# Phase 1 of a bidirectional scan layer: two scan operands per tile and store, with other places for three intermediates

## The chip, the cores and the metric

The kernel runs on one core of a Trainium2 chip. The metric is device time in microseconds of one execution. A core has TensorE (matrix products, into the accumulator memory PSUM), VectorE, ScalarE and GpSimd for elementwise work on the on-chip memory SBUF, and SyncE, which here issues most of the DMA transfers. Each engine has its own queue of instructions; they wait for one another by semaphores.

## What is computed

One layer for 128 context tokens and 2048 latent tokens of width 1024. A normalised and modulated input `h` goes through one projection to r, k, v and gate channels (group A, 8 heads of 64) and to the four inputs of a gated convolution (group B). Group A is a delta-rule scan in both directions:

```
kk = k * kk_scale / norm;  kd = k * (1 + (a - 1) * ka_scale)
S  = S * w_t - (S kk_t) (kk_t * a_t)^T + v_t k_t^T ;   y_t = S r_t
y  = groupnorm(y_fwd + y_bwd) * gn_w + gn_b + bonus * v,   bonus = sum(r * kd * bonus_rk)
out = x + gate * ([y * silu(g_a), yb] @ w_out)
```

The decay `w` and the rate `a` differ per direction and come from two small low-rank products of `h`. The outputs are the normalised results and the final states of the context.

## The kernel before

There are three phases, all written for one core. Phase 1 makes everything that depends on one token block alone and writes it to DRAM; phase 2 runs the scan in chunks of 64 tokens; phase 3 does the output projection. The Tile framework takes the program's tiles, gives them places in SBUF and decides the order of the instructions on each engine from a simulated timeline; waits follow from the tiles. A tile names a pool, a tag and a number of places (`bufs`); the tiles of one tag take turns in its places, and a new tile waits until the last reader of the old one, a store among them, is done.

**Phase 1** (`phase1`, lines 50 to 644) takes the 2176 tokens in six blocks (five of 384, one of 256), two blocks at a time: three "thirds" (`THIRD`, the loop at line 571). In each third the weights are walked once: for each of four groups of 128 channels, `turn(0, ...)` runs `mixA` on both blocks and `turn(1, ...)` runs `gateA`, with the convolution's `convB` and `gateB` between them. Each product is made of three matmuls per 128 input channels, with weights and inputs split into a high and a low part (`products`, lines 158 to 162).

`load_w` (line 117) brings a weight column block. The first time it loads raw weights into a place of tag "wr" (pool `wp`, 2 places of 4 KB in each partition), ScalarE and VectorE split them, and the two parts are stored to DRAM (`scr_wsp`); in the later thirds both parts are loaded from there, 1 MB at a time (line 121), so "wr" is used in the first third only. `gate_rows` (line 528) uses it there too.

`mixA` (lines 337 to 411) makes, for one channel group and token block, the shifted k (line 345) and r (line 356, through `shifted`, lines 313 to 330, in which ScalarE empties the product's PSUM place at lines 319 and 321 and GpSimd adds neighbours at line 323), the normalised k (lines 346 to 355, with a sum over the heads by `part_sum`), and then for each direction d the four operands of the scan: al (line 387), rh (line 390), ka (line 398) and be (lines 401 and 402). Each of the four is a tile [128, 384] of tag "sp", which has four places, and each has a store of its own through `spill` (line 332), issued by SyncE into one of four planes of the DRAM tensor `ops0` or `ops1`. The bonus sum over both directions ends in a tile "bsum" (lines 405 to 410).

`gateA` (lines 413 to 444) makes the shifted v (line 418), transposes it on TensorE (line 422) and writes it less its head mean into a tile "vt" (one place, line 423; line 432), stored at line 433. The low part in `parts_of` (line 195) has the same tag "vt". Then comes the gate sg, and the term q = (bonus * v + bias) * sg, in another "sp" tile (lines 441 to 443), with a store.

At the end of the third third, phase 1's pools on the right side are closed (line 632) and phase 2's first tiles take their room: `early` (line 1153) loads masks, makes the operand tiles rr (preset at line 787) and loads the scan operands of the first two stages (line 868), with the initial states ahead of them (line 948). The convolution's last two groups run beside it.

Of the kernel before, what the change touches and what calls it, by code (L numbers as in the profile page):

```python
# [6 lines left out]
F32 = mybir.dt.float32  # L7
# [9 lines left out]
BLK = [(0, 384), (384, 384), (768, 384), (1152, 384), (1536, 384), (1920, 256)]  # L17
# [10 lines left out]

OPS = dict(al0=0, rh0=1, ka0=2, be0=3, be1=0, ka1=1, rh1=2, al1=3)


class Ctx:
# [15 lines left out]
def phase1(K):  # L50
    nc, tc, A, S = K.nc, K.tc, K.A, K.S
    V, G, P, T = nc.vector, nc.gpsimd, nc.scalar, nc.tensor
    cp = Pool(K, "p1c", "left")
    wp = Pool(K, "p1w", "left", 2)
# [4 lines left out]
    ta_ = Pool(K, "p1ta", "right")  # L59
# [36 lines left out]
    def vcol(i):  # L96
        return vec[:, i:i + 1]
# [15 lines left out]
                up[n, d] = (hi[:, n, d], lo[:, n, d])  # L113

    kept = set()

    def load_w(cb):

        w = wp.tile([128, 2, 8, 128], F32R, tag="w", name=f"w{cb}_{K.u()}", bufs=4)
        if cb in kept:  # L120
            nc.sync.dma_start(w[:].bitcast(F32), S["wsp"][cb])
            return w
        raw = wp.tile([128, 8, 128], F32, tag="wr", name=f"wr{cb}_{K.u()}", bufs=2)
        nc.sync.dma_start(raw[:], A["win"][cb])
        P.copy(w[:, 0], raw[:])
        V.tensor_tensor(w[:, 1], raw[:], w[:, 0].bitcast(F32), ALU.subtract)
        nc.sync.dma_start(S["wsp"][cb], w[:].bitcast(F32))
        kept.add(cb)
        return w
# [23 lines left out]
    def dense(w, hh, n, nm):  # L153
        ps = pmm.tile([128, 384], F32, tag="mm", name=f"mm{nm}_{K.u()}")
        products(ps, w, hh, n, range(8))
        return ps
# [174 lines left out]

    def spill(name, g, j, t_, nm):
        t0, n = BLK[j]
        dst = S[f"ops{name[2]}"][OPS[name]] if name in OPS else S[name]
        nc.sync.dma_start(dst[g * 128:(g + 1) * 128, t0:t0 + n], t_[:, :n])

    def mixA(g, j, ws, hh, lw, pre):

        t0, n = BLK[j]
        nch = n // 64  # L340
        tl = lambda tag, b=1: (tp if tag == "sg" else ta_).tile([128, 384], F32, tag=tag, name=f"{tag}_{g}_{j}_{K.u()}", bufs=b)
        wk, wr_ = ws
        psk, psr = pre or (None, None)

        kS = shifted(psk or dense(wk, hh, n, "k"), j, 1, g, "k", 1)
        sq = tl("sq")
        P.activation(sq[:, :n], kS[:, :n], AF.Square, scale=vcol(V_KK + g))
        pss = part_sum(onr, sq, n, f"s{g}_{j}")
        n2 = sq
        V.tensor_scalar(n2[:, :n], pss[:, :n], 1e-24, None, ALU.max)  # L350
        V.reciprocal(n2[:, :n], n2[:, :n])
        kk = tl("kk")
        P.activation(kk[:, :n], kS[:, :n], AF.Identity, scale=vcol(V_KK + g))
        kkn = n2
        V.tensor_tensor(kkn[:, :n], kk[:, :n], n2[:, :n], ALU.mult)
        rS = shifted(psr or dense(wr_, hh, n, "r"), j, 0, g, "r", 1)
        kds = []
        for d in range(2):
            cs = slice(g * 128, g * 128 + 128)

            def lup(which):
                ps = pmm.tile([128, 384], F32, tag="mm", name=f"up{which}_{K.u()}")
                hi, lo = up[which, d]
                x = lw[which * 2 + d]
                T.matmul(ps[:, :n], hi[:, cs], x[:, :n], start=True, stop=False)
                T.matmul(ps[:, :n], lo[:, cs], x[:, :n], start=False, stop=True)
                return ps

            psw = lup(0)
            t = tl("t", 2)  # L370
            P.activation(t[:, :n], psw[:, :n], AF.Tanh, bias=dcol(D_W0H + d * 4 + g), scale=0.5)
            V.tensor_scalar(t[:, :n], t[:, :n], -0.5 * DEC, -0.5 * DEC, ALU.mult, ALU.add)
            c = t
            if d == 0:
                V.tensor_tensor_scan(c[:, :n], smask[:, :n], t[:, :n], 0.0, ALU.mult, ALU.add)
            else:
                V.tensor_tensor_scan(c[:, :n][:, ::-1], smask[:, :n], t[:, :n][:, ::-1], 0.0, ALU.mult, ALU.add)
            pt = rot(pp[d], "pp")
            c3 = c[:, :n].rearrange("p (a b) -> p a b", b=64)
            P.activation(pt[:, :nch, 1 - d:65 - d], c3, AF.Exp)  # L380
            P.activation(c[:, :n], c[:, :n], AF.Exp, bias=nln2[:], scale=-1.0)
            psa = lup(1)
            ta = tl("ta", 2)
            P.activation(ta[:, :n], psa[:, :n], AF.Tanh, bias=dcol(D_IBH + d * 4 + g), scale=0.5)
            v3 = lambda x_: x_[:, :n].rearrange("p (a b) -> p a b", b=64)
            al = tl("sp", 4)
            V.tensor_tensor(v3(al), v3(kk), pt[:, :nch, d:64 + d], ALU.mult)
            spill(f"al{d}", g, j, al, "al")
            rh = tl("sp", 4)
            V.tensor_tensor(v3(rh), v3(rS), pt[:, :nch, 1 - d:65 - d], ALU.mult)  # L390
            spill(f"rh{d}", g, j, rh, "rh")
            nc.scalar.dma_start(S[f"pc{d}"][g * 128:(g + 1) * 128, t0 // 64:t0 // 64 + nch], pt[:, :nch, 64 - 64 * d])

            kd = tl("kd", 2)
            P.activation(kd[:, :n], ta[:, :n], AF.Identity, bias=dcol(D_KA2 + g), scale=vcol(V_KA + g))
            V.tensor_tensor(kd[:, :n], kd[:, :n], kS[:, :n], ALU.mult)
            kap = tl("sp", 4)
            V.tensor_tensor(kap[:, :n], kd[:, :n], c[:, :n], ALU.mult)
            spill(f"ka{d}", g, j, kap, "kap")
            be = tl("sp", 4)  # L400
            V.scalar_tensor_tensor(be[:, :n], ta[:, :n], 1.0, kkn[:, :n], ALU.add, ALU.mult)
            V.tensor_tensor(be[:, :n], be[:, :n], c[:, :n], ALU.mult)
            spill(f"be{d}", g, j, be, "be")
            kds.append(kd)
        bs = kds[0]
        V.tensor_tensor(bs[:, :n], kds[0][:, :n], kds[1][:, :n], ALU.add)
        V.scalar_tensor_tensor(bs[:, :n], bs[:, :n], dcol(D_RKQ + g), rS[:, :n], ALU.mult, ALU.mult)
        psb = part_sum(onr, bs, n, f"b{g}_{j}")
        bsum = tl("bsum", 2)
        P.copy(bsum[:, :n], psb[:, :n])  # L410
        return bsum

    def gateA(g, j, ws, hh, bsum):

        t0, n = BLK[j]
        tl = lambda tag, b=1: (tp if tag == "sg" else ta_).tile([128, 384], F32, tag=tag, name=f"{tag}_{g}_{j}_{K.u()}", bufs=b)
        wv, wg = ws
        vS = shifted(dense(wv, hh, n, "v"), j, 2, g, "v", 1)

        psv = pax.tile([128, 3, 128], F32, tag="ax", name=f"psv{g}_{j}")  # L420
        for i in range(n // 128):
            T.transpose(psv[:, i, :], vS[:, i * 128:(i + 1) * 128], idt[:])
        vt = ta_.tile([128, 3, 128], F32, tag="vt", name=f"vt{g}_{j}", bufs=1)

        c0 = 1 if lat_off(j) else 0
        if c0:
            P.copy(vt[:, 0], psv[:, 0])
        heads = lambda x: x[:, c0:n // 128].rearrange("p i (h c) -> p i h c", h=2)
        m = n // 128 - c0
        mn = ta_.tile([128, 3, 2], F32, tag="vmean", name=f"vmean{g}_{j}", bufs=1)  # L430
        V.tensor_reduce(mn[:, :m], heads(psv), mybir.AxisListType.X, ALU.add)
        V.scalar_tensor_tensor(heads(vt), mn[:, :m].unsqueeze(3).broadcast_to((128, m, 2, 64)), -1.0 / 64, heads(psv), ALU.mult, ALU.add)
        nc.sync.dma_start(S["vt"][t0:t0 + n, g * 128:(g + 1) * 128].rearrange("(a p) c -> p a c", p=128), vt[:, :n // 128])

        psg = dense(wg, hh, n, "g")
        tg = tl("sg", 2)
        P.activation(tg[:, :n], psg[:, :n], AF.Tanh, scale=0.5)
        sg = tg
        V.scalar_tensor_tensor(sg[:, :n], tg[:, :n], 1.0, psg[:, :n], ALU.add, ALU.mult)
        spill("sg", g, j, sg, "sg")  # L440
        q = tl("sp", 4)
        V.tensor_tensor(q[:, :n], bsum[:, :n], vS[:, :n], ALU.mult)
        V.scalar_tensor_tensor(q[:, :n], q[:, :n], dcol(D_GBH + g), sg[:, :n], ALU.add, ALU.mult)
        spill("q", g, j, q, "q")
# [120 lines left out]
    def coming(j, j2):  # L565

        yield from norm_steps(j, load_x(j))
        yield from make_h(j, xb[j])
        yield from norm_steps(j2, load_x(j2))

    for t3, js in enumerate(THIRD):
        wd, wi = wlora if t3 == 0 else (load_w(32), load_w(33))
        lws, pre, conv, sums = {}, {}, {}, {}
        more = coming(*THIRD[t3 + 1]) if t3 < 2 else iter(())
        WA, WB = ((4, 0), (8, 12)), ((20, 24), (28, 16))
        early = gate_rows() if t3 == 0 else iter(())
# [837 lines left out]
```

## Time and profile before

| | us |
|---|---|
| median of three runs | 1746.37 |
| lowest and highest of the three | 1745.83, 1748.89 |
| span of the profiled execution, first to last instruction | 1752.9 |
| TensorE busy in that span | 1647.9 (94%) |
| VectorE busy | 1093.0 (62%) |
| ScalarE busy | 870.1 (50%) |
| GpSimd busy | 582.1 (33%) |

The profile was taken on one execution; its page gives the span and no other time for it, and the span is 6.5 us above the median of the runs. Times in the profile's rows count from the start of that span. The borders of the thirds lie near 390 and 717 us, and phase 2's first products are at 943 us. In a row of a timeline stand the start, the duration, the engine, the line, the operation and the tiles (written <- read), and in brackets the idle time of the engine before it and what ended that. In a row of waits stand who waited and for whom, the sum in us, how often, and the longest. In a row of windows stand the stretch, its length, the busy time (and number of instructions) of TensorE, its weight loads, VectorE, ScalarE and GpSimd, and then the granted clock of TensorE as a share of full speed, the busy share of the DMA engines, and GB/s.

### The profile page before, as it was taken

The page shows a single profiled execution, that of the slowest core. Times are in us where ns is not written, and L with a number is a line of the kernel's source. Part 1 is how long each engine was busy: PE and PEld are TensorE (multiplying, and loading weights), DVE is VectorE, ACT ScalarE, POOL GpSimd, SP SyncE. Part 2 cuts the span into 40 slices and gives each one's busy share as a digit, 9 for nine tenths or more (in the row PEclk, how much of TensorE's full clock was granted, in tenths as well). Part 3 has the DMA queues.
Part 4 walks back from the last instruction along what each step waited for, and adds up shares of the span by engine and source line. Part 5 has one row for each costly group of instructions (what it writes and reads, how often), then busy time and mean ns, then how long its engine had stood idle before and what let it go on. Part 6 is the DMA issues. An engine that isn't in the chain of part 4 may idle for free. (4 is left out here: it accounts for less than half of the span.)

```text
span 1752.9 us, 33041 instructions
## 1 busy us (share of the span) xinstructions
PE 1647.9 (94%) x12400; PEld 1558.8 (89%) x12400; DVE 1093.0 (62%) x2092; ACT 870.1 (50%) x1719; POOL 582.1 (33%) x1089
## 2 busy tenths in 40 slices
PE   5999899998999999999998989999999999899998
PEld 2889898998999998999998979899999999787886
DVE  5875788866567766567764544475776666656333
ACT  4534455534143433334442367687788787633222
POOL 0011111111011101011120587777777778223221
PEclk9899999999999999999999998899999999999999
DMA  9797778785557646477666585587677875746442
GB/s 367 208 234 220 233 241 246 232 255 151 148 160 227 169 147 174 135 258 217 195 214 225 173 196 135 141 192 187 174 198 189 191 185 120 180 151 206 151 144 90
DMA packets 315825, 335.69 MB, mean 192 GB/s; under 512 B 166985, under 2 KB 263881, under 8 KB 301585
## 3 DMA queue, kind: packets, MB, share of 16 engines
q1 hardware_dynamic: 243360, 324.52, 62.6%
q10 hardware_dynamic: 70944, 4.60, 2.9%
q0 software_dynamic: 1360, 4.46, 0.7%
q8 instruction: 98, 1.61, 0.4%
q14 instruction: 63, 0.51, 0.1%
HBM read 221.42 MB, written 112.08 MB: 190 GB/s over the span
## 5 line engine op out<-in xcount | busy, mean ns | idle before, releaser
L934 POOL TENSOR_TENSOR zt<-zt,ztmp 128x30 f32<-128x30 f32 (+7 forms) x510 | 197.3, 387 | 39.3
L1054 PE MATMUL psS<-sv,E 128*128 128x64 f32 x1088 | 155.1, 277 | 1.0 <-DVE sv L1067 0.6
L1029 PE MATMUL psE<-str,stl 128*128 128x128 f32 x1088 | 144.1, 281 | 11.3 <-DVE E L1030 7.0
L1054 PEld LDWEIGHTS psS<-sv,E 128*128 128x128 f32 x1088 | 145.4, 200 | 3.3 <-DVE sv L1067 0.8
L1029 PEld LDWEIGHTS psE<-str,stl 128*128 128x128 f32 x1088 | 131.8, 194 | 14.1 <-DVE E L1030 7.9
L931 POOL TENSOR_TENSOR ztmp<-ab,zt 128x60 f32<-128x60 f32 (+7 forms) x255 | 130.8, 513 | 19.2
L1067 DVE TENSOR_TENSOR sv<-psS,pc 64x128 f32<-64x128 f32 x254 | 69.2, 277 | 92.9 <-PE psS L1054 92.2
L779 ACT COPY bd<-rr 64x512 f32<-64x512 f32 x136 | 84.0, 617 | 75.7 <-DMA rr<-scr_ops 23.3
L323 POOL TENSOR_TENSOR shk<-rawl 128x384 f32<-128x384 f32 (+1 forms) x24 | 20.7, 861 | 291.9 <-ACT rawl L319 291.9
L1030 DVE TENSOR_TENSOR E<-psE,msk 128x512 f32<-128x512 f32 x136 | 92.7, 684 | 33.0 <-PE psE L1029 32.3
L892 PE MATMUL psF<-rr,bd 128*128 128x128 f32 x544 | 80.0, 295 | 16.2 <-ACT Q L779 9.8
L892 PEld LDWEIGHTS psF<-rr,bd 128*128 128x128 f32 x544 | 70.7, 203 | 20.4 <-ACT Q L779 12.9
L1350 POOL TENSOR_TENSOR z<-z,x 128x512 f32<-128x512 f32 x32 | 43.6, 1364 | 126.6 <-DVE z L1346 105.9
L1018 PE MATMUL psX<-F,zb 128*128 128x128 f32 x544 | 78.2, 297 | 3.2 <-ACT zb L777 2.3
L197 POOL TENSOR_TENSOR hslb<-kd,hshb 128x384 fp32r<-128x384 f32 (+1 forms) x24 | 26.7, 1113 | 164.0 <-ACT hshb L196 143.5
L160 PE MATMUL mmc<-h,w 128*128 128x384 f32 (+1 forms) x192 | 67.9, 354 | 13.4 <-ACT q1r L321 9.8
L323 POOL TENSOR_TENSOR shv<-rawl 128x384 f32<-128x384 f32 (+1 forms) x24 | 25.4, 1060 | 153.4 <-ACT rawl L319 153.4
L892 PE MATMUL psG<-rr,bd 128*128 128x128 f32 x544 | 72.0, 280 | 4.4 <-DVE F L893 4.4
L1018 PEld LDWEIGHTS psX<-F,zb 128*128 128x128 f32 x544 | 71.6, 209 | 4.0 <-POOL zt L934 1.9
L892 PEld LDWEIGHTS psG<-rr,bd 128*128 128x128 f32 x544 | 65.7, 193 | 5.0 <-DVE F L893 4.8
L161 PE MATMUL mmc<-h,w 128*128 128x384 f32 (+1 forms) x192 | 66.1, 344 | 0.0
L162 PE MATMUL mmc<-h,w 128*128 128x384 f32 (+1 forms) x192 | 65.7, 342 | 0.0
(307 smaller groups left out, 5205.4 us busy)
## 6 DMA issues: line engine op xcount, KB each, us to landing
w<-scr_wsp SPq DMA_DIRECT2D x68, 1024.0 KB, 7.3
scr_wsp<-w SPq DMA_DIRECT2D x34, 1024.0 KB, 6.0
rr<-scr_ops SPq DMA_DIRECT2D x64, 512.0 KB, 4.6
scr_ops<-sp SPq DMA_DIRECT2D x160, 192.0 KB, 5.2
wr<-in_win SPq DMA_DIRECT2D x34, 512.0 KB, 6.3
ab<-scr_at SPq DMA_DIRECT2D x34, 256.0 KB, 4.2
x<-in_x SPq DMA_DIRECT2D x17, 512.0 KB, 3.8
wadas<-in_wada SPq DMA_DIRECT2D x8, 1024.0 KB, 13.0
```

The source lines that it names most:

```text
L160: T.matmul(ps[:, :n], w[:, 0, k], hh[:, 0, k, :n], start=k == 0, stop=False)
L161: T.matmul(ps[:, :n], w[:, 0, k], hh[:, 1, k, :n], start=False, stop=False)
L162: T.matmul(ps[:, :n], w[:, 1, k], hh[:, 0, k, :n], start=False, stop=k == 7)
L779: (V.tensor_copy if k in ON_DVE else P.copy)(dst, src)
L892: T.matmul(ps[:, i, :].rearrange("p (a b) -> p a b", b=64), w[:, u, :], x[:, :, u, :], start=True, stop=True)
L931: G.tensor_tensor(tv, ab[:, j:j + 2, j + 2:32].unsqueeze(1).broadcast_to((128, kn, 2, n)), zt[:, :kn, j:j + 2].unsqueeze(3).broadcast_to(( ...
L934: G.tensor_tensor(zt[:, :kn, j + 2:32], zt[:, :kn, j + 2:32], tv[:, :, r], ALU.subtract)
L1018: T.matmul(px[:, i, :], B.zb[:, gi, us.start + i, :], g.F[:, us.start + i, :], start=True, stop=True)
L1029: T.matmul(pe[:, i, hd, :].rearrange("p (b t) -> p b t", b=2), g.lt[:, :, hd, us.start + k + i].rearrange("p b t -> p (b t)"), g.rt[:, :, ...
L1030: V.tensor_tensor(g.E[n][:, k:k + 2].rearrange("p a b c -> p (a b) c"), pe[:].rearrange("p a b c -> p (a b) c"), B.msk[:, ME[g.d]].unsquee ...
L1054: T.matmul(sp[gi][:, q, hd, :], g.E[n][:, k, hd, :], sv[:, u, hd, :], start=True, stop=True)
L1067: r = V.tensor_tensor(dst, sp[gi][0:64, q], B.pc[0:64, d, 2 * p:2 * p + 2, c:c + 1].broadcast_to((64, 2, 64)), ALU.mult)
```

## The change

The four scan operands of a direction become two tiles [128, 2, 384], a pair of al and rh and a pair of ka and be, each with one store that writes two neighbouring planes of `ops0` or `ops1`. The halves of a pair are ordered by direction so that the planes are the same as before. Tag "sp" has two places of pairs, which take the room of the four single ones. q is written into bsum's tile in place. From the second third on (`late`), every other pair, which is the al/rh pair of each direction, is a tile of tag "wr" in the pool `wp`, and so is the transposed v (two places for both). No arithmetic changes.

```diff
+    late = []
...
     def spill(name, g, j, t_, nm):
         t0, n = BLK[j]
-        dst = S[f"ops{name[2]}"][OPS[name]] if name in OPS else S[name]
-        nc.sync.dma_start(dst[g * 128:(g + 1) * 128, t0:t0 + n], t_[:, :n])
+        nc.sync.dma_start(S[name][g * 128:(g + 1) * 128, t0:t0 + n], t_[:, :n])
+
+    npair = [0]
+
+    def pair():
+
+        npair[0] += 1
+        nm = f"pair{npair[0]}"
+        if late and npair[0] % 2:
+            return wp.tile([128, 2, 384], F32, tag="wr", name=nm, bufs=2)
+        return ta_.tile([128, 2, 384], F32, tag="sp", name=nm, bufs=2)
+
+    def spill2(d, k, g, j, t_):
+        t0, n = BLK[j]
+        nc.sync.dma_start(S[f"ops{d}"][k:k + 2, g * 128:(g + 1) * 128, t0:t0 + n].rearrange("k p t -> p k t"), t_[:, :, :n])
...
-            al = tl("sp", 4)
+            ar = pair()
+            al, rh = ar[:, d], ar[:, 1 - d]
             V.tensor_tensor(v3(al), v3(kk), pt[:, :nch, d:64 + d], ALU.mult)
-            spill(f"al{d}", g, j, al, "al")
-            rh = tl("sp", 4)
             V.tensor_tensor(v3(rh), v3(rS), pt[:, :nch, 1 - d:65 - d], ALU.mult)
-            spill(f"rh{d}", g, j, rh, "rh")
+            spill2(d, 2 * d, g, j, ar)
...
-            kap = tl("sp", 4)
+            kb = pair()
+            kap, be = kb[:, d], kb[:, 1 - d]
             V.tensor_tensor(kap[:, :n], kd[:, :n], c[:, :n], ALU.mult)
-            spill(f"ka{d}", g, j, kap, "kap")
-            be = tl("sp", 4)
             V.scalar_tensor_tensor(be[:, :n], ta[:, :n], 1.0, kkn[:, :n], ALU.add, ALU.mult)
             V.tensor_tensor(be[:, :n], be[:, :n], c[:, :n], ALU.mult)
-            spill(f"be{d}", g, j, be, "be")
+            spill2(d, 2 - 2 * d, g, j, kb)
...
-        vt = ta_.tile([128, 3, 128], F32, tag="vt", name=f"vt{g}_{j}", bufs=1)
+        vt = (wp if late else ta_).tile([128, 3, 128], F32, tag="wr" if late else "vt", name=f"vt{g}_{j}", bufs=2 if late else 1)
...
-        q = tl("sp", 4)
+        q = bsum
         V.tensor_tensor(q[:, :n], bsum[:, :n], vS[:, :n], ALU.mult)
...
+        if t3:
+            late.append(t3)
```

More of the change, by code (lines that the diff above doesn't have):

```diff
@@ L27 @@
 ND = 68
-OPS = dict(al0=0, rh0=1, ka0=2, be0=3, be1=0, ka1=1, rh1=2, al1=3)
 class Ctx:
```

## The prediction

> **What bounds the kernel now.** I read the page first, then the table of windows over the three thirds of phase 1, then the waits of VectorE and TensorE in them, and last the timelines around the longest TensorE gaps.
>
> ```profile
> span 1752.9 us, 33041 instructions
> ...
> PE 1647.9 (94%) x12400; PEld 1558.8 (89%) x12400; DVE 1093.0 (62%) x2092; ACT 870.1 (50%) x1719; POOL 582.1 (33%) x1089
> ```
>
> TensorE is busy for 94% of the span, so a gain can only be TensorE idle time, or time at a lower clock. The change touches phase 1 alone, which ends near 940 us. Its thirds, with TensorE first after the length, and granted clock, DMA share and GB/s last:
>
> ```profile
> 60.00:390.00 330.00, 312.51 (x1704) 295.87 (x1703) 248.96 (x440) 151.55 (x285) 44.89 (x42) 0.97 0.80 233
> 390.00:717.00 327.00, 312.09 (x1762) 308.78 (x1761) 204.75 (x372) 117.08 (x235) 41.95 (x42) 0.98 0.59 174
> 717.00:930.00 213.00, 209.38 (x1413) 207.49 (x1412) 139.54 (x280) 83.03 (x189) 37.07 (x48) 1.00 0.65 201
> ```
>
> TensorE idles 17.5, 14.9 and 3.6 us. VectorE has room, but waits for the stores that free its four "sp" places. First third, then the other two:
>
> ```profile
> DVE sp L387 <- DMA scr_ops<-sp: 17.3, 6, 5.0
> DVE sp L401 <- DMA scr_ops<-sp: 6.1, 3, 3.5
> DVE sp L390 <- DMA scr_ops<-sp: 2.4, 3, 1.4
> ```
>
> ```profile
> DVE t L372 <- ACT t L371: 33.3, 10, 3.6
> DVE ok L329 <- POOL shk L323: 24.5, 7, 4.6
> DVE sp L387 <- DMA scr_ops<-sp: 20.0, 6, 6.7
> DVE sp L401 <- DMA scr_ops<-sp: 19.5, 11, 2.9
> DVE sp L398 <- DMA scr_ops<-sp: 10.0, 5, 3.6
> ```
>
> That is 25.8 us and 49.5 us of VectorE waiting. What TensorE waited for, first third and then the others:
>
> ```profile
> PE pss L204 <- ACT hshs L196: 4.9, 3, 3.9
> ...
> PE psb L204 <- ACT hshb L196: 1.2, 1, 1.2
> ```
>
> ```profile
> PE mmc L160 <- ACT q1r L321: 9.6, 4, 4.9
> PE psb L204 <- ACT hshb L196: 3.4, 1, 3.4
> ...
> PE pss L204 <- ACT hshs L196: 1.3, 2, 0.9
> ```
>
> ScalarE is named, but it is not the cause. Followed back, the longest gap reads:
>
> ```profile
> 428.25 0.56 DVE L398 TENSOR_TENSOR sp<-kd,t 128x384 f32<-128x384 f32 x1 [1.60 <-DMA scr_ops<-sp]
> 429.74 0.56 DVE L401 SCALAR_TENSOR_TENSOR sp<-ta,sq 128x384 f32<-128x384 f32 x1 [0.93 <-DMA scr_ops<-sp]
> ```
>
> ```profile
> 430.87 0.61 ACT L347 ACTIVATE sq<-ok,vec 128x384 f32<-128x384 f32 x1 [4.78 <-DVE ok L329]
> ```
>
> ```profile
> 432.88 0.69 PE L160 MATMUL mmc<-h,w 128*128 128x384 f32 x1 [4.87 <-ACT q1r L321]
> ```
>
> VectorE stands twice on a store, so `ok` is late; ScalarE runs its queue in order (square, scaled copy, then the copies that empty r's PSUM bank), so the next product has no bank. I followed the other gaps of the three rows back in the same way; they led to an L387, L398 or L401 wait as well.
>
> Why are stores slow to land? The issue list gives size and median time to landing:
>
> ```profile
> w<-scr_wsp SPq DMA_DIRECT2D x68, 1024.0 KB, 7.3
> ...
> rr<-scr_ops SPq DMA_DIRECT2D x64, 512.0 KB, 4.6
> scr_ops<-sp SPq DMA_DIRECT2D x160, 192.0 KB, 5.2
> ```
>
> A 192 KB store takes longer than a 512 KB load of two rows: it lands when the megabytes of weights ahead of it on the same queue have.
>
> Each gap also costs clock. Around the gaps named, with TensorE's granted clock third from the end:
>
> ```profile
> 178.00:190.00 12.00, 7.96 (x32) 7.48 (x32) 9.36 (x19) 8.74 (x18) 2.08 (x2) 0.72 0.75 276
> ...
> 286.00:296.00 10.00, 8.26 (x38) 7.61 (x37) 7.76 (x16) 2.73 (x6) 1.76 (x1) 0.84 0.95 364
> ...
> 430.00:440.00 10.00, 7.12 (x32) 7.12 (x33) 7.36 (x13) 8.27 (x17) 2.47 (x2) 0.83 0.71 221
> ```
>
> A stretch of 10 us at 0.83 lost 1.7 us. The other two long gaps of the second third (at 517 and 689) have a stretch of half clock like it, taken at the same price as an estimate: 5.1 us in the three.
>
> **The change, part by part.**
>
> *Two later thirds: four pairs.* From the second third on, the al/rh pairs go to the two "wr" places and the ka/be pairs keep the two of "sp": eight halves for four. The next writer of a place comes a whole block later, not half a block. Each third has eight blocks (four channel groups, two token blocks), so one every 27 us or more on average (213/8), though the two of a turn stand closer; with 5.2 us for a store I cost the sp waits of these thirds at nothing. The cover is that distance; if it were gone we are back at the old waits. The idle time behind them is 9.6 + 3.4 + 1.3 = 14.3 us. What is late next is ScalarE's tanh (L372's row) and GpSimd's shift sum (L329's), both of which belong to the chain of a block's start; I let them keep a fifth. So 11.5 us of idle and four fifths of the clock, 4 us: **−15.5 us**. Bounds: −19.4 (all of it) and −5 (the waits go, the gaps stay mostly).
>
> The Trainium skill, "TensorE: Matmul & The Clock Gate", Part 1, says that the clock is gated in windows of 3413 ns at half rate after an idle window. By it a gap costs 1.7 us of matmul time whatever its own length, three of them 5.1 us; the 0.83 over 10 us agrees.
>
> *The end of phase 1: the transposed v.* Its one place "vt" becomes the two "wr" places, in a pool that phase 2's first loads don't overlap; q moves from "sp" into bsum's place. Before:
>
> ```profile
> 928.66 0.42 DVE L432 SCALAR_TENSOR_TENSOR vt<-vmean,psv 128x256 f32<-128x256 f32 x1 [4.31 <-DMA scr_vt<-vt]
> 935.80 0.76 DVE L787 COPY rr<-I 128x512 f32<-128x512 f32 x2 [6.72 <-DMA scr_vt<-vt]
> ```
>
> ```profile
> SPq L948 <- DMA scr_q<-sp: 5.8, 1, 5.8
> ```
>
> ```profile
> 929.11 0.37 SPq L433 DMA_DIRECT2D scr_vt<-vt  x1
> 935.38 0.52 SPq L948 DMA_DIRECT2D st<-in_st  x1
> 936.08 1.99 SPq L868 DMA_DIRECT2D rr<-scr_ops  x4
> ```
>
> ```profile
> 943.16 1.19 PE L892 MATMUL psF<-rr,bd 128*128 128x128 f32 x4 [5.88 <-DMA rr<-scr_ops]
> ```
>
> The last v block waits for the first one's store, the preset of phase 2's operand tile waits for the last one's, the state load ahead of the operand loads on SyncE's queue waits for q's, and TensorE pays 5.88 us. Both holders move, so the loads could go some 6 us earlier; two weight loads of 1 MB are still ahead of them, at 7.3 us. I take half of the gap and 1 us of clock: **−4 us**, bounds 0 and −8. If q's store now holds back another phase 2 tile on bsum's place, it is 0.
>
> *First third: two pairs.* "wr" is still in use for raw weights, so four single places become two of pairs. The al/rh pair of the second direction waits for a store issued one VectorE instruction later than before, which is +0.5 us where it waits (six times, 3 us). Worse is the other pair: ka of the second direction used to go into any single place that was free; now it needs a whole pair, and the ka/be pair of the first direction is full only after its second product:
>
> ```profile
> 289.77 0.55 DVE L402 TENSOR_TENSOR sp<-sp,t 128x384 f32<-128x384 f32 x1
> ...
> 291.17 0.55 DVE L398 TENSOR_TENSOR sp<-kd,t 128x384 f32<-128x384 f32 x1
> ```
>
> The first row completes that pair at 290.3; with the 5.2 us of a store it lands at 295.5 by estimate, and the second row, ka of the second direction at 291.17, would start 4.3 us later. That happens once in each of eight blocks: 0 to 34 us of new VectorE waiting. The queue behind it is whatever the scheduler has interleaved (at 291 the convolution's taps), and ScalarE and TensorE wait for that. Price for TensorE: the 25.8 us of the first third's sp waits stand behind 4.9 + 1.2 us of idle and 3.4 + 1.6 us of clock (0.72 over 12 us, 0.84 over 10), about 0.4 us for each. I take 9 us from the ka pairs (a quarter of the bound, since the scheduler can place the write later) and 3 from the al pairs: 12 × 0.4 = **+5 us**, bounds −1 (fewer issues) and +15.
>
> The Trainium skill, "DMA: Bandwidth & Descriptors", Anatomy of one DMA, says that a transfer costs about 2.0 us fixed and its bytes at 436 GB/s. By it, as an estimate, a pair's store lands in 2.9 us against 2.5 for a single one, and the new wait would be near 2 us where I put 4.3; the trace's 5.2 us for 192 KB differs, since these stores queue.
>
> *Small.* q in bsum's place: its writer stands where it stood, and the next bsum copy comes a block and more later, so its cover is that distance; 0. SyncE issues 96 two-row stores for 192, as the operand loads already do; its queue is off the path; 0. A merged store is one VectorE instruction later in SyncE's queue, and the weight loads behind it with it: 0.5 us against loads made four places ahead; 0.
>
> **Sum.** −15.5 − 4 + 5 = −14.5 us. The profiled execution's span, 1752.9, lies 6.5 us above the runs' median of 1746.37; 0.4% of these terms is under 0.1 us, so I take the sum off the median: **1732 us**. Its own range, from half the first gain to all of both with no loss: 1719 to 1742.
>
> **Rivals.**
> *The gaps refill.* TensorE's gaps at a block's start have other late comers, 33.3 us of waits for the tanh and 24.5 us for the shift sum; if these come up to where the sp waits were, the first term is −5, the second −2, and the first third takes +5: 1744 us, no change. For it: those rows are longer than the sp rows. Against: at 432.88 VectorE's two waits make half of the gap by themselves.
> *The first third turns it.* Two pair places in the stage with the highest DMA share (0.80) and the busiest VectorE (249 of 330 us): with all bounds at their bad ends, −5 + 0 + 15 = +10: 1756 us. It decides once new VectorE waiting there is over 19.5/0.4 = 49 us (some 6 us a block), or less where the gains fall short. Against it: the scheduler may place the blocked write behind other work.
> *Stores land by their own size.* If a pair's place comes free 2 us after its second half, the first third costs +1, not +5, and both gains stand in full, 19.4 + 6: 1722 us. For it: in quiet stretches stores do land faster. Against: the 5.2 us row.
> *The late places aren't there.* vt and the al/rh pairs share two places; were each pair to meet a v store, the first term halves; this lies inside the forecast's range.
>
> **How the numbers follow.** Forecast 0.55, refill 0.20, first third 0.15, fast stores 0.10. Within 0.2%, about what a measurement of this kernel can tell from no change, is 1742.9 to 1749.9. Faster: the forecast, nearly all, the fast stores, and some of refill: 0.67. Same: the rest of refill and a sliver of the forecast: 0.16. Slower: 0.17. The range takes the fast stores' case and the bounds down to 1717, and goes up past refill to 1750; the bad end of the first third is left out.
>
> **What would show it.** Right: no L387 or L398 wait for a store after 400 us, the gaps at 432, 517, 593 and 688 gone, TensorE's idle time in the two later thirds under 8 us, clock 0.99 there; operand loads at the end of phase 1 right behind the weight loads and the first psF gap under 3 us; in the first third longer waits of L398. Wrong: sp waits of over 45 us in the first third with TensorE idle over 30 us there, or the same idle in the later thirds under other names.

## The result, and the profile after

The changed kernel takes 1731.63 us in the median of four runs (1725.37 to 1736.05), against 1746.1 for four of the kernel before (1745.32 to 1748.89); the medians are 14.5 us apart. The ratio is 0.9894, 95% interval 0.9864 to 0.9924: faster by 18.5 us of 1746, at least 13 and at most 24. In two later comparisons it is 0.9901 (0.9867 to 0.9935) and 0.9875 (0.9848 to 0.9902). The kernel before itself was at 1736.9, 1737.6 and 1751.7 us in later comparisons, on three different chips, so times are set side by side within one comparison only.

The page of the changed kernel, first lines:

```profile
span 1728.5 us, 32831 instructions
...
PE 1643.7 (95%) x12400; PEld 1558.1 (90%) x12400; DVE 1102.0 (64%) x2092; ACT 869.9 (50%) x1719; POOL 585.0 (34%) x1089
```

The same work stands in a shorter span. The table of windows over the thirds of phase 1, the first length after the stretch being followed by TensorE's busy time:

```profile
60.00:390.00 330.00, 312.27 (x1681) 296.53 (x1680) 248.56 (x438) 150.90 (x284) 44.73 (x42) 0.96 0.78 228
390.00:717.00 327.00, 324.07 (x1863) 322.40 (x1862) 215.96 (x384) 119.56 (x241) 42.52 (x43) 1.00 0.63 183
717.00:930.00 213.00, 208.28 (x1424) 206.94 (x1423) 148.74 (x289) 85.02 (x193) 39.73 (x47) 0.99 0.70 223
```

In the second stretch TensorE's idle time went from 14.9 to 2.9 us and its clock from 0.98 to 1.00. (The third stretch now holds the start of phase 2, so its idle time isn't that of the third.) What VectorE waited for, first third, and then the other two:

```profile
DVE pair L401 <- DMA scr_ops<-pair: 27.6, 8, 5.0
...
DVE pair L411 <- DMA scr_ops<-pair: 0.3, 1, 0.3
```

```profile
DVE t L385 <- ACT t L384: 36.6, 14, 3.6
DVE ok L329 <- POOL shk L323: 28.3, 8, 5.3
...
DVE pair L411 <- DMA scr_ops<-pair: 0.3, 1, 0.3
```

L401 writes al, L411 writes ka. After 390 us 49.5 us of store waits have become 0.3. VectorE waits some 7 us more for the tanh and the shift sum instead, and little of that reaches TensorE. Its own waits there:

```profile
PE mmc L160 <- ACT q1r L321: 2.7, 3, 2.0
PE up L378 <- DVE lw L573: 2.5, 1, 2.5
PE psF L905 <- DMA rr<-scr_ops: 2.2, 1, 2.2
```

The row for the PSUM bank of r is down from 9.6 to 2.7, and the 3.4 us for the bonus sum are gone. At the end of phase 1, VectorE, SyncE and TensorE:

```profile
909.68 0.42 DVE L443 SCALAR_TENSOR_TENSOR vt<-vmean,psv 128x256 f32<-128x256 f32 x1
910.02 0.76 DVE L800 COPY rr<-I 128x512 f32<-128x512 f32 x2
```

```profile
911.64 0.48 SPq L334 DMA_DIRECT2D scr_q<-bsum  x1
912.22 0.60 SPq L444 DMA_DIRECT2D scr_vt<-vt  x1
912.91 1.35 SPq L961 DMA_DIRECT2D st<-in_st  x1
914.35 5.38 SPq L881 DMA_DIRECT2D rr<-scr_ops  x4
```

```profile
924.09 2.02 PE L905 MATMUL psF<-rr,bd 128*128 128x128 f32 x16 [2.20 <-DMA rr<-scr_ops]
```

Neither the last v block nor the preset waits, and SyncE issues the state load and the operand loads right after v's store. TensorE waits 2.20 us where it waited 5.88.

The lengths of the stages, read from the timelines: each third from its first low-rank product (mml) to the next third's, the last one to the first psF product, and phase 2's main part from there to the last psS product.

| profile | first third | second | third and hand-over | phase 2 | gap before psF |
|---|---|---|---|---|---|
| before | 341.1 | 326.3 | 226.4 | 645.4 | 5.9 |
| changed | 345.1 | 308.8 | 221.4 | 639.9 | 2.2 |

That is +4.0, −17.5 and −5.0 us in phase 1, −18.5 together. Another 5.5 us come from phase 2, which the change doesn't touch; a second profile of the kernel before, below, bears on them.

### The profile page after: what moved, and what is told of

Read it like the earlier page. It is cut to its first block, busy times and chain, and to the rows that moved or that the text cites. A ratio compares the mean times of both kernels' runs of the same rounds, so it can differ in the third digit from the quotient of the medians.

```text
span 1728.5 us, 32831 instructions
## 1 busy us (share of the span) xinstructions
PE 1643.7 (95%) x12400; PEld 1558.1 (90%) x12400; DVE 1102.0 (64%) x2092; ACT 869.9 (50%) x1719; POOL 585.0 (34%) x1089
## 5 line engine op out<-in xcount | busy, mean ns | idle before, releaser
L323 POOL TENSOR_TENSOR shk<-rawl 128x384 f32<-128x384 f32 (+1 forms) x24 | 25.6, 1066 | 334.6 <-ACT rawl L319 321.9
L905 PEld LDWEIGHTS psF<-rr,bd 128*128 128x128 f32 x544 | 69.0, 199 | 17.3 <-ACT Q L792 14.1
L905 PE MATMUL psG<-rr,bd 128*128 128x128 f32 x544 | 75.5, 289 | 4.2 <-DVE F L906 4.2
L160 PE MATMUL mmc<-h,w 128*128 128x384 f32 (+1 forms) x192 | 68.8, 358 | 6.3 <-ACT ta L397 2.9
L905 PEld LDWEIGHTS psG<-rr,bd 128*128 128x128 f32 x544 | 69.2, 202 | 4.6 <-DVE F L906 4.4
L161 PE MATMUL mmc<-h,w 128*128 128x384 f32 (+1 forms) x192 | 67.6, 352 | 0.0
L162 PE MATMUL mmc<-h,w 128*128 128x384 f32 (+1 forms) x192 | 67.3, 350 | 0.0
L906 DVE TENSOR_TENSOR F<-psF,msk 128x512 f32<-128x512 f32 x68 | 46.7, 688 | 28.4 <-PE psF L905 15.7
```

The source lines that it names most:

```text
L160: T.matmul(ps[:, :n], w[:, 0, k], hh[:, 0, k, :n], start=k == 0, stop=False)
L161: T.matmul(ps[:, :n], w[:, 0, k], hh[:, 1, k, :n], start=False, stop=False)
L162: T.matmul(ps[:, :n], w[:, 1, k], hh[:, 0, k, :n], start=False, stop=k == 7)
L905: T.matmul(ps[:, i, :].rearrange("p (a b) -> p a b", b=64), w[:, u, :], x[:, :, u, :], start=True, stop=True)
```

## The experiments

Theory: the second and third thirds gain by having places for twice as many operands; q and v give the hand-over; two pair places cost the first third a little. Rivals: merging the stores carries the gain; q's and v's places do; the first third's loss is scatter.

**The changed kernel again.**

> The changed kernel once more, beside the other kernels of this call. My theory: in phase 1 the first third is some 4 us longer than before (345 against 341 us), the second some 17 us shorter, the third with the hand-over to phase 2 some 5 us shorter, and these lengths come back within 2 us. Phase 2 was 5.5 us shorter in the first profile, which no term of the prediction covers; if that is the changed order of its instructions it comes back, if it is chance it does not. Time 1727 to 1735 us.

1720.13 us, ratio 0.9901 (0.9867 to 0.9935). The thirds: 340.3, 309.8 and 221.0 us. The second and the last came back within 1 us, the first did not: 345.1 and 340.3 us for the same program. Phase 2 took 635.5. The time is under the 1727 to 1735 us expected, but in this comparison the kernel before is lower too (1736.9).

**Single places in the first third.**

```diff
-            ar = pair()
-            al, rh = ar[:, d], ar[:, 1 - d]
+            if late:
+                ar = pair()
+                al, rh = ar[:, d], ar[:, 1 - d]
+            else:
+                al = tl("sp", 4)
...
-            kb = pair()
-            kap, be = kb[:, d], kb[:, 1 - d]
+            kap = tl("sp", 4)
...
+            be = tl("sp", 4)
```

Each single tile has its own store; in `pair` every tile is of tag "wr". ka and be keep the four single places in the later thirds too, so the first third isn't all that differs from the changed kernel.

> First third as before (four single places, four stores), later thirds with the al/rh pair in the raw weights' places, ka and be in the four single places, q and v as in the change. Theory (two pair places cost the first third 4 us): the first third is back at 341 us, the rest stays, time 3 to 5 us below the changed kernel. Rival (the order of phase 1 as a whole shifts and the first third's length is chance, or the waits only move): the first third stays within 2 us of the changed kernel's and the time is the same.

1711.07 us, ratio 0.9859 (0.9827 to 0.989), 9 us below the changed kernel in the same comparison. First third 335.8 us against 340.3, second 309.1, last 219.5. VectorE's store waits in the first third:

```profile
DVE sp L406 <- DMA scr_ops<-sp: 14.5, 6, 4.1
...
DVE sp L424 <- DMA scr_ops<-sp: 4.0, 3, 1.7
```

L406 writes al, L424 be: with the row of 0.6 us left out here 19.1 us, against 27.2 for al and 2.7 for ka in the changed kernel of the same comparison. The first third gained 4.5 us, as the theory had it, but both stand 5 us below the lengths that it named, and the time fell by 9 us, not 3 to 5. Of the 13.4 us between the two profiles, 6.7 lie in phase 2, which took 628.8 us.

**Pairs only.**

```diff
-        if t3:
-            late.append(t3)
```

> Pairs and q in bsum's place, but the raw weights' places are never used later: two pair places in all three thirds, v in its single place. Theory (the gain comes from the number of places): the later thirds lose their gain and pay what the first third pays; second third 328 us or more, time 1746 to 1758 us, slower than before or no better. Rival (the gain comes from merging two stores into one): second third at 312 us or less and time near 1735 us.

1738.29 us, ratio 1.0016 (0.999 to 1.0042): no gain at all. Second third 328.9 us; the first is 338.8 us, not longer, where the theory had it paying for its pairs. The window of the second third, and the store waits after 390 us:

```profile
390.00:717.00 327.00, 310.11 (x1747) 307.39 (x1746) 204.14 (x369) 117.34 (x235) 40.26 (x42) 0.98 0.57 171
```

```profile
DVE pair L411 <- DMA scr_ops<-pair: 22.6, 13, 3.6
...
DVE pair L401 <- DMA scr_ops<-pair: 21.8, 9, 6.2
```

With the merged stores in place, 44 of the 49.5 us of waits and all of the idle time (17 us) are back.

**All places, two stores for each pair.**

```diff
             V.tensor_tensor(v3(al), v3(kk), pt[:, :nch, d:64 + d], ALU.mult)
+            spill1(d, 3 * d, g, j, al)
             V.tensor_tensor(v3(rh), v3(rS), pt[:, :nch, 1 - d:65 - d], ALU.mult)
-            spill2(d, 2 * d, g, j, ar)
+            spill1(d, 1 + d, g, j, rh)
```

(`spill1` stores one half into one plane; the same for ka and be.)

> All places as in the change, but each half of a pair is stored by itself as soon as it is written (192 stores again). Theory (places, not merging): time within 3 us of the changed kernel. Rival (fewer and larger stores carry the gain, through SyncE's queue): the second third is 5 us or more longer and the time 1737 us or more.

1724.88 us, ratio 0.9925 (0.9894 to 0.9956); the second third has 311.3 us, 1.5 more than the changed kernel. The median is 4.8 us above the changed kernel's, more than the theory's 3 and far from the rival's 1737, and the intervals of the two ratios overlap widely. So the places carry the gain; what merging adds is 1.5 us in the second third of one profile, and not resolved in the time.

**The kernel before again.**

> The kernel before, once more with a profile. The first third is 341 us in the one profile of it, and 340 and 339 us in two kernels with two pair places, so the loss of 4 us that the prediction gave the pairs may not be there. Theory (pairs cost the first third): 334 to 337 us here. Rival (they cost it nothing, and the 336 us of the kernel with single places and q in bsum's place come from q): 339 to 342 us. Second third 325 to 329 us, gap before the first psF product 5 to 7 us. Phase 2 was 645 us in the first profile and 629 to 640 us in five others; if that is chance it lies anywhere between.

1740.82 us, ratio 1.0019 (0.9994 to 1.0044). The thirds are 341.3, 325.5 and 224.4 us, near its first profile; the gap is 4.54 us, under the 5 to 7 expected. The first third came out as the rival had it, not the theory: with its four single places it is as long as in some kernels with pairs. Phase 2 took 637.3 us instead of 645.4. The same program is thus 8.1 us apart there, more than the 5.5 us between the first two profiles, which can be chance; in thirteen profiles of nine programs phase 2 runs from 629 to 645 us.

**v back in its single place.**

```diff
-        vt = (wp if late else ta_).tile([128, 3, 128], F32, tag="wr" if late else "vt", name=f"vt{g}_{j}", bufs=2 if late else 1)
+        vt = ta_.tile([128, 3, 128], F32, tag="vt", name=f"vt{g}_{j}", bufs=1)
```

> The change with the transposed v left in its single place. Theory (v's place sets the hand-over): the last v block waits 4 us for the first one's store again, phase 2's operand loads come later and TensorE's gap before the first psF product is 4 to 6 us against 2; the third with the hand-over is 3 to 4 us longer, the second third stays at 309 to 312 us. Rival (q's place set it, through the state load ahead of the operand loads): the gap stays at 2 us.

1719.73 us, ratio 0.989 (0.986 to 0.9919), no slower than the change. The waits of the prediction's chain are back:

```profile
912.18 0.42 DVE L443 SCALAR_TENSOR_TENSOR vt<-vmean,psv 128x256 f32<-128x256 f32 x1 [5.53 <-DMA scr_vt<-vt]
916.40 0.76 DVE L800 COPY rr<-I 128x512 f32<-128x512 f32 x2 [3.81 <-DMA scr_vt<-vt]
```

but TensorE's gap is no longer than in the change:

```profile
921.57 2.02 PE L905 MATMUL psF<-rr,bd 128*128 128x128 f32 x16 [2.00 <-ACT bd L792]
```

The third with the hand-over takes 222.2 us against 221.0 to 222.7 in the change. So the gap stayed, as the rival had it. But v's place does hold the loads back, as SyncE's waits and its queue show:

```profile
SPq L881 <- DMA scr_vt<-vt: 2.7, 1, 2.7
```

```profile
907.92 0.45 SPq L334 DMA_DIRECT2D scr_q<-bsum  x1
...
916.46 1.91 SPq L881 DMA_DIRECT2D rr<-scr_ops  x4
```

The operand loads are issued 8.5 us after q's last store, where the change has 2.7 (911.64 to 914.35). TensorE didn't pay for it here: its other products lasted until 11.7 us after that store (10.2 in the change), and the loads landed at least 4.6 us after their issue (8.0 in the change).

**v and q alone**, and **v alone**, with four single places all along.

```diff
+    late = []
...
-        vt = ta_.tile([128, 3, 128], F32, tag="vt", name=f"vt{g}_{j}", bufs=1)
+        vt = (wp if late else ta_).tile([128, 3, 128], F32, tag="wr" if late else "vt", name=f"vt{g}_{j}", bufs=2 if late else 1)
...
-        q = tl("sp", 4)
+        q = bsum
...
+        if t3:
+            late.append(t3)
```

> The kernel before with v in the raw weights' places in the later thirds and q in bsum's place; four single places with their four stores all along. Theory: second third 325 to 329 us as before (the scan operands' places are what counts there), gap before psF 2 to 3 us. First third: 334 to 337 us if q's place helps it, 339 to 342 us if not. Time 3 to 6 us below before. Rival (v's and q's places carry the gain of the second third): 312 us there.

1731.52 us, ratio 0.9945 (0.9923 to 0.9967). Second third 324.8, as before; last third 220.2, gap 2.67; first third 338.6, in neither of the two ranges expected. Here the operand loads are issued 1.7 us after q's last store.

> The kernel before with v alone in the raw weights' places in the later thirds; q in one of the four single places. Theory (v and q each hold one of the hand-over's loads back): the state load still waits for q's store, so the gap before psF stays at 4 us or more. Rival (v alone): gap 2 to 3 us. Second third 325 to 329 us by both.

(Without the two lines on q.) 1738.15 us, ratio 0.9991 (0.997 to 1.0011). Second third 325.3, last third 222.7, first third 338.6. SyncE and TensorE:

```profile
SPq L951 <- DMA scr_q<-sp: 6.7, 1, 6.7
```

```profile
935.49 3.76 PE L895 MATMUL psF<-rr,bd 128*128 128x128 f32 x16 [4.82 <-ACT ct L456]
```

With q in "sp", the state load waits 6.7 us at the head of SyncE's queue for q's store, and the operand loads stand behind it: they are issued 8.2 us after that store. (The last row names ScalarE, whose copy from rr just before had waited for the operand load.) In the three profiles with q in "sp" the gap is 5.9, 4.5 and 4.8 us; in the ten with q in bsum's place it is 4.0 at most and under 3 in eight. The length of the third doesn't separate them: 222.7 us here, 221.0 to 222.7 in the change. v and q alone are worth 0.3 to 0.8% of the time and nothing in the second third. As to the first third, q didn't help it: 338.6 us with it and without, and both are 2.6 us under the kernel before, which has the same places there.

**Singles first and the changed kernel once more, and one pair place.**

> The kernel with single places in the first third and the changed places later, once more, beside the changed kernel on one chip. First profiles: first third 336 us against 345, 340, 339 and 340 in four kernels with pairs there. Theory (pairs cost the first third a few us): 336 to 338 us again, and the time 3 us or more below the changed kernel. Rival (the lengths of this third scatter by 4 us, and phase 2, 629 us in the first profile, was a lucky one): 338 to 342 us and a time within 3 us of the changed kernel.

1719.92 us, ratio 0.9812 (0.9787 to 0.9837). First third 339.8 us: not the theory's 336 to 338 but inside the rival's range, and 4.0 us from the same program's first profile. The time, though, is 10.8 us below the changed kernel's, as the theory had it and not the rival, and the first third is 6.7 us below the one in the next run, its partner.

> The changed kernel as the partner of that run: first third 339 to 345 us, second third 309 to 310, third with the hand-over 221, phase 2 629 to 640 us by chance.

1730.71 us, ratio 0.9875 (0.9848 to 0.9902). First third 346.5 us, over the range expected, second 309.8, last 222.7, phase 2 631.3 against 630.5 in the partner. The first third's waits of the two, the changed kernel first:

```profile
DVE pair L401 <- DMA scr_ops<-pair: 28.3, 8, 5.9
```

```profile
DVE sp L406 <- DMA scr_ops<-sp: 16.5, 6, 4.0
...
DVE sp L424 <- DMA scr_ops<-sp: 3.4, 3, 1.5
```

```diff
-        return ta_.tile([128, 2, 384], F32, tag="sp", name=nm, bufs=2)
+        return ta_.tile([128, 2, 384], F32, tag="sp", name=nm, bufs=1)
```

> The change with one place of tag sp for pairs in place of two, which in the first third makes every pair wait for the store of the one before it (32 pairs). It gives the price of VectorE's waiting in TensorE's time there. Theory (0.4 us of the third for each us of store waits, as the prediction priced it): with some 100 to 150 us of new waits the first third is 40 to 60 us longer. Rival (VectorE has the room, a third of its time is free, and little of it comes through): under 20 us longer. Later thirds: the ka/be pairs alone alternate with one place, so some 5 to 15 us of the gain of the second third goes.

One run: 1742.6 us, where the kernel before had 1751.68. First third 350.7 us, 4.2 more than with two places; second 319.4. Store waits up to 400 us:

```profile
DVE pair L411 <- DMA scr_ops<-pair: 28.4, 10, 7.0
...
DVE pair L401 <- DMA scr_ops<-pair: 3.0, 2, 2.0
```

Not 100 to 150 us of new waits, but 31.4 in all where two places had 28: presumably the scheduler put the writes that find no place later, behind other work. So the price of a wait in TensorE's time couldn't be measured this way and stays open. For the second third the row of the theory held: with one place for the ka/be pairs, 10 of the 17 us are lost.

## Why the prediction was right, point by point

**What bounds the kernel:** right. In phase 1 TensorE's idle time and clock moved. Between the second third's own borders 12 of the 17.5 us are idle time (14.9 to 2.9) and the rest is shorter busy time (311.4 to 305.9 us for the same products) at a higher clock: the stretch from 430 to 440 us, at 0.83 before, is at 1.00 after.

**Later thirds, −15.5 us:** the mechanism was right, the term a little small. The second third alone gave 17.5 us (16 to 17 in the other comparisons), and the last third 1.3 beside its gap (5.0 less 3.7), which is less than the 2.0 us between the kernel before's two profiles: 18.8 at most, where the bound was 19.4. The fifth that was kept for the tanh and the shift sum was wrong: VectorE's waits for these did grow, by 3.3 and 3.8 us, but TensorE's idle time there is 2.9 us. "Pairs only" shows that the places are the cause and "two stores" that merging isn't; "v and q alone" rules these out for the second third.

The Trainium skill's half-rate windows of 3413 ns ("TensorE: Matmul & The Clock Gate", Part 1) had put three gaps at 5.1 us of clock, as an estimate; the second third's 17.5 less 12.0 us of idle time leaves 5.5. What the prediction made of it, a price for a gap whatever its length, isn't borne out: before, the gaps of 4.87, 2.54 and 3.38 us in the second third each brought 3.4 us at half clock and the one of 3.88 us at 178 brought 6.8, but one of 1.77 us (at 593), and in the changed kernel one of 1.97 us (at 432.94), brought none.

**Hand-over, −4 us:** the gap lost 3.7 us. "Both holders move" was right for the loads: after q's last store their issue takes 2.7 us with both moved, 8.5 with v back, 8.2 with q back and 7.9 before. What TensorE paid doesn't follow from that alone. With v back the gap is 2.00 us, with q back 4.8; it also depends on how long other products last and how soon the loads land, so the price is in part luck.

**First third, +5 us:** the mechanism was wrong, and that the size came near is luck. First profiles +4.0; against single places in the same comparison, +4.5 and +6.7 (and −1 in the one where the kernel before itself was the partner and v's place differed). Over all, six profiles with four single places there took 335.8 to 341.3 us and six with two pair places 338.8 to 346.5, so whether pairs cost this third anything isn't settled. The failed step is "ka of the second direction at 291.17 would start 4.3 us later", priced at 9 us of waits: the scheduler moved that write, as the prediction allowed, and its row is 0.3 us (0.3 to 3.7 in the six). In the changed kernel's timeline:

```profile
176.45 0.56 DVE L401 TENSOR_TENSOR pair<-kk,pp 128x384 f32<-128x384 f32 x1 [4.97 <-DMA scr_ops<-pair]
...
178.32 0.55 DVE L413 TENSOR_TENSOR pair<-pair,t 128x384 f32<-128x384 f32 x1
...
180.11 0.55 DVE L411 TENSOR_TENSOR pair<-kd,t 128x384 f32<-128x384 f32 x1
```

ka (last row) comes after the first direction's be is done, without a wait. The al pair waits longer, 27.6 us in eight waits where al had 17.3 in six: +10 where the prediction had +3. But the waits of rh and be, 8.5 us before, are gone, so VectorE's store waits in this third went from 26.4 to 27.9 us, +1.5 in all and not +12. TensorE's idle time between the third's borders hardly moved either (18.7 to 19.0 us); the other 3.7 of the 4.0 us are longer busy time at a lower clock, to which the last section comes back.

A pair's store takes longer to land than a single one's 5.2 us:

```profile
scr_ops<-pair SPq DMA_DIRECT2D x80, 384.0 KB, 7.2
```

That isn't why al waits more often. With the same places and a store for each half ("two stores"), al still waits eight times:

```profile
scr_ops<-pair SPq DMA_DIRECT2D x160, 192.0 KB, 5.2
```

```profile
DVE pair L405 <- DMA scr_ops<-pair: 24.4, 8, 4.5
```

So the rival in which stores land by their own size is out; in the changed kernel the sixteen stores of 256 KB took 9.2 us. By the Trainium skill's fixed 2.0 us and 436 GB/s ("DMA: Bandwidth & Descriptors", Anatomy of one DMA, a fit for transfers that GpSimd issues; these are SyncE's) a pair's store would have taken 2.9 us, as an estimate. What the rest of the 7.2 us is isn't shown: the prediction's reason, megabytes of weights ahead on the queue, was not tested.

**What would show it:** after 400 us 0.3 us of store waits, TensorE's idle time 2.9 and 4.7 us in the two later thirds (between their own borders), the clock 1.00 and 0.99, a gap of 2.20 us before psF, as named. Not as named: a gap of 1.97 us is left at 432.94, and the waits of ka (L398, now L411) in the first third didn't grow.

**The sum:** −14.5 us forecast; phase 1 gave −18.5 in the first two profiles, the ratio says −18.5 with 13 to 24 in its interval. The difference of the medians, 14.5, agrees to the digit with the forecast by chance: the four runs of the changed kernel scatter by 11 us. That the first third's +5 fits is luck, and so is a part of the hand-over's −4.

**A version that beats both:** single places in the first third, and later the al/rh pair in the raw weights' places with ka and be in single ones: 0.9859 and 0.9812 of the kernel before where the changed kernel has 0.9901 and 0.9875. In the second the intervals don't meet. The profiles are 13.4 and 8.1 us apart, of which the first third has 4.5 and 6.7; in the one 6.7 lie in phase 2, which scatters by itself, and in the other 1.2 in the last third. As the first third scatters too, the cause of this version's gain isn't shown.

## What to carry to other kernels

A wait of TensorE that names ScalarE can be a store two engines back: follow it to the first wait for a DMA before costing it. Where a store queues behind megabytes of loads, count places by time to landing, not by bytes: twice the places took 49.5 us of waits to 0.3, while merged stores in the same room gave nothing. At a change of phase, look for the load at the head of the queue whose place an old store still holds; it delays all behind it, though TensorE pays only if it has no other products by then.

## What was not expected of the hardware

The same program's first third took 345.1, 340.3 and 346.5 us in three profiles, while its second third took 308.8, 309.8 and 309.8. The difference is clock. Beside the row of the first profile above, with a clock of 0.96, the other two read:

```profile
60.00:390.00 330.00, 311.90 (x1708) 296.36 (x1708) 249.59 (x440) 151.61 (x285) 47.69 (x42) 0.98 0.79 234
```

```profile
60.00:390.00 330.00, 309.92 (x1673) 293.55 (x1672) 249.38 (x438) 150.69 (x283) 44.89 (x42) 0.96 0.78 226
```

In the traces TensorE's granted clock is either full or half, and the half-rate stretches last 3.4 us or a multiple of it. Half of their time is lost: 13.9, 7.4 and 14.0 us in these three first thirds, without which they are 331.2, 332.9 and 332.5 us long. The six profiles with four single places lose 5.7 to 9.2 us and are 329.5 to 332.0 us long without it. On average the six with pairs are 3.2 us longer, and 2.4 of that is time at half clock. So most of this third's scatter, and most of what pairs seem to cost in it, is clock; why it comes in one execution and not in another isn't shown.

The kernel before ran at 1746, 1737, 1738 and 1752 us in four comparisons, a spread nearly as large as the gain.
